# Rebuilding the head of a two-layer hybrid diffusion trunk on one core: load order, sum of squares, place of the first filter

## The chip, the core and the metric

The kernel runs on one core of one Trainium2 chip. The core has TensorE (PE in the profile; its weight loads are PEld), VectorE (DVE), ScalarE (ACT), GpSimd (POOL) and SyncE (SP), and 16 DMA engines. The metric is the device time of one launch in microseconds, the median of several runs. The whole program is one launch with fixed inputs.

## The reference, cut to what matters

Two layers work on `x` and on a context `xc`, each 256 tokens of 1024 features. The second layer leaves the context as it is.

```python
def layer_forward(x, xc, mod, mod_c, lp, update_ctx):
    sh1, sc1, g1, sh2, sc2, g2 = split(mod, 6)            # mod = silu(c) @ ada_w + ada_b
    h = modulate(rmsnorm(x, norm1_g), sh1, sc1)           # modulate: x * (1 + scale) + shift
    p = h @ w_in                                          # the context goes the same way
    attn = neighborhood_attention(q, k, v, kc, vc, rpb)   # 8 heads, softmax over 512 keys
    x = x + g1 * merge_branches(p, attn, lp)
    h = modulate(rmsnorm(x, norm2_g), sh2, sc2)
    x = x + g2 * conv_ffn(h, lp)

def merge_branches(p, attn, lp):
    a = spatial_gating_mixer(p[..., :1024])
    hy = hyena_mixer(p[..., 2560:4096])                   # two long convolutions by spectra
    g_a, g_b, g_c = split(sigmoid(p[..., 4096:]), 3)
    return (g_a * (a @ wb[0]) + g_b * (attn @ wb[1]) + g_c * (hy @ wb[2])) @ w_out

def hyena_filter_spectrum(...):
    h = sin(freq * (z @ w1 + b1)); h = sin(freq * (h @ w2 + b2))
    h = (h @ w3) * decay                                  # k: both directions
    return rfft(k / sum(abs(k)))
```

## The kernel before, in words

Activations are stored with features on the 128 partitions and tokens along the free axis: `xT` is 8 tiles of 128x512, x in columns 0 to 255 and the context in 256 to 511. Every product of layer activations and weights is done three times, with weights and activations each split in a high and a low part (`wp`, `hh`/`hl`): lines L311 to L313, or L316 to L319 where several tiles share one row of weights. The splits of weights are made some parts ahead, the high part by ScalarE (L251) and the low one by VectorE (L258). Tiles come from a pool of 77 units of 128x512, taken by `U()`; a unit taken again waits until its last reader is done.

Nothing reorders the program: each engine runs its instructions in the order in which the code issues them. Weight chunks are used one after the other in a list; after each feature tile, `pump` runs a fixed number of steps from a side queue, in which work of other parts waits as generators: the filters' spectra, spatial gating, attention, hyena. `step(g)` runs a generator to its next `yield`; `br_split` drains what a branch needs at once before its products start (spatial gating for branch 0, attention for 1, hyena for 2; their order is 0, 2, 1). Names that the text uses: `S` are attention's scores, `P` the softmax, `PT` and `PTs` its transposes and their copies, `pv` the products with the values; `Ze`/`Zo` are hyena's forward transforms, `P`, `T`, `Pp`, `Tp`, `yr`, `yi` its spectra on VectorE, `y` and `yT` its inverse transforms; `fh` are the filter's last layer, `fps` its sine layers, `nsum` its norm.

The head is `first()`. It loads x, then what the first filter needs, then the first norm's modulation weights in four groups `aw[k, c]` of 8 tiles, with weight chunks between. It squares x on ScalarE (L1241), adds the squares on POOL and VectorE (L1244), sums over partitions by four matmuls (`ssum`, L1257), takes 1/rms (L1261 and behind), spreads it over all partitions (`rb`, L1268), and forms shift and scale group by group (`gemv`, L1276 to L1286) and the normed tiles (`norm`, L1293 to L1298). Steps of the first filter are placed by hand between these. The first four feature tiles are multiplied row by row as the normed tiles come.

Of the kernel before, what the change touches and what calls it, by code (L numbers as in the profile page):

```python
# [60 lines left out]
def constants():  # L61
# [13 lines left out]
    for p in range(128):  # L75
        q = p % 64
        half, i = (q % 32) // 16, q % 16
        a = (cols if half else rows) * inv_freq[i]
        k[p, K_COS:K_COS + L] = np.cos(a)
        # rotate-half's sign comes with the sine  # L80
        k[p, K_SIN:K_SIN + L] = np.sin(a) * (-1.0 if q < 32 else 1.0)
# [12 lines left out]
def trunk_kernel(ctx: ExitStack, tc: tile.TileContext, A: dict, out: bass.AP):  # L94
# [14 lines left out]
    def fm(name, n, T, dt=F32):  # L109
        """n feature tiles of T tokens."""  # L110
# [31 lines left out]
    nc.sync.dma_start(out=prm, in_=A["prm"])  # L142
    nc.sync.dma_start(out=kst[0:33, K_POS:K_POS + 256], in_=A["kst"][0:33, K_POS:K_POS + 256])
# [31 lines left out]
    def split(src, hi, lo):  # L175
        """src = hi + lo, both with the 12 significant bits that one pass carries."""
# [12 lines left out]
    def evacuate(g):  # L189
        """an evacuation in stages: the first now, one more with each further piece of weights"""  # L190
        if g is not None and step(g):
            stages.append(g)
# [16 lines left out]
    def cuts(kind, kt, ncols):  # L209
        """a chunk's pieces in the order of their use, each cut into parts of one unit (rows k0:k1, columns c0:c1):  # L210
        a feature tile a piece (m), or all of it (t)"""
# [10 lines left out]
    def run_items():  # L222
# [39 lines left out]
        def prime(n):  # L262
            """splits n parts ahead of the next chunk"""
# [11 lines left out]
        for i, it in enumerate(items):  # L275
# [14 lines left out]
            def piece(j, more=True, i=i, qs=qs):  # L290
                """the j-th piece's rows, each in two parts; splits further parts ahead"""
# [14 lines left out]
    def mm_k(outs, W, R, k, s0, s1, n):  # L306
        """outs[i] += W[i][k]^T R[k][:, s0:s1], W and R in two parts, k of n; R's low part comes last"""
# [13 lines left out]
    def fm_run(tiles, R, s0, s1, mid=None):  # L321
        """feature tiles (W, evac, m) of one segment, side by side over the rows; mid runs ahead of their evacuation"""
# [12 lines left out]
    def fm_chunk(R, segs, evac, nm=2):  # L335
        """use() of a chunk of nm feature tiles: evac(m, ps, s0, s1) takes each."""
# [1114 lines left out]
```

## Time and profile before

| | us |
|---|---|
| three runs | 1458.31, 1463.16, 1462.58 |
| median | 1462.58 |
| span of the profiled execution | 1459.6 |
| TensorE busy | 1417.0 (97%) |
| VectorE busy | 1010.6 (69%) |
| ScalarE busy | 662.8 (45%) |
| GpSimd busy | 92.0 (6%) |

The profiled execution is known by its span alone, from its first to its last instruction. All times of rows count from the start of that span. Busy time of an engine leaves out register, branch, semaphore and DMA-issuing instructions. In rows of the timeline, a bracket such as [1.98 <-ACT hh L1295] gives the idle time of the engine ahead of the instruction and what ended it.

### The profile page before, as it was taken

What the parts mean: (1) busy time and instruction counts of PE and PEld (TensorE: products, weight loads), DVE (VectorE), ACT (ScalarE), POOL (GpSimd) and SP (SyncE); (2) the same over time, 40 slices, a digit from 0 to 9 for tenths busy, and PEclk for the clock granted to TensorE, in tenths of its full rate; (3) what the DMA queues carried; (4) which work ended last, traced back from release to release, by engine and by line L of the source; (5) the groups of instructions that cost most, each with busy time, mean ns of one, the idle gap of its engine ahead of it and who ended that gap; (6) DMA issues with size and microseconds to landing.
All of it is one profiled execution on the core that took longest, in us unless ns stands there. A gap on an engine that the chain in (4) does not pass through costs nothing.

```text
span 1459.6 us, 22459 instructions
## 1 busy us (share of the span) xinstructions
PE 1417.0 (97%) x8902; PEld 1222.7 (84%) x8902; DVE 1010.6 (69%) x1872; ACT 662.8 (45%) x1382; POOL 92.0 (6%) x96
## 2 busy tenths in 40 slices
PE   4999999999999999999999999999999999999997
PEld 3887777767878889988878787899789899999997
DVE  5736844676775566667978899587667787776574
ACT  4443332434664435533322433365436765665352
POOL 1010201010000000000011120000020000000000
PEclk9999999999999999999999999999999999999998
DMA  9934435334221523334488635535333455555642
GB/s 314 302 123 151 138 125 185 109 104 134 80 87 58 188 87 107 99 134 153 137 248 260 200 121 166 175 125 167 105 116 107 154 159 190 171 175 173 200 140 66
DMA packets 194533, 220.21 MB, mean 151 GB/s; under 512 B 5531, under 2 KB 182716, under 8 KB 189308
## 3 DMA queue, kind: packets, MB, share of 16 engines
q1 hardware_dynamic: 189420, 206.97, 43.8%
q0 software_dynamic: 2896, 9.18, 2.0%
q10 hardware_dynamic: 2112, 2.62, 0.7%
q8 instruction: 70, 1.15, 0.3%
q14 instruction: 35, 0.29, 0.1%
HBM read 215.61 MB, written 1.05 MB: 148 GB/s over the span
## 4 chain that ended last, share of the span: by engine, by line
PE 86%; DVE 7%; DMA 3%; ACT 2%; issue 1%; SPq 0%; ACTq 0%; POOL 0%; DVEq 0%; POOLq 0%
PE mm L311 23%; PE mm L313 23%; PE mm L312 23%; DVE wp L258 2%; DMA aw<-ada_w 2%; PE mt L941 2%; PE mt L943 2%; PE mt L942 2%; PE pv L815 1%; PE PT L803 1%; PE S L783 1%; PE ada L382 1%; PE Ze L643 1%; PE Zo L644 1%; PE mm L316 1%
## 5 line engine op out<-in xcount | busy, mean ns | idle before, releaser
L311 PE MATMUL mm<-hl,wp 128*128 128x256 f32 (+1 forms) x1476 | 501.1, 340 | 0.8 <-DVE hl L485 0.7
L313 PE MATMUL mm<-hh,wp 128*128 128x256 f32 (+1 forms) x1476 | 492.3, 334 | 0.0
L312 PE MATMUL mm<-hh,wp 128*128 128x256 f32 (+1 forms) x1476 | 491.9, 333 | 0.0
L258 DVE TENSOR_TENSOR wp<-w,wp 128x512 fp32r<-128x512 f32 (+1 forms) x576 | 374.6, 693 | 28.1 <-ACT wp L251 25.6
L251 ACT CAST wp<-w 128x512 fp32r<-128x512 f32 (+1 forms) x576 | 321.3, 610 | 85.8 <-DMA w<-ffn_w_down 35.5
L311 PEld LDWEIGHTS mm<-hl,wp 128*128 128x128 f32 x1476 | 281.1, 190 | 37.7 <-issue 6.6
L312 PEld LDWEIGHTS mm<-hh,wp 128*128 128x128 f32 x1476 | 281.1, 190 | 28.9 <-issue 2.9
L313 PEld LDWEIGHTS mm<-hh,wp 128*128 128x128 f32 x1476 | 280.9, 190 | 28.2 <-DVE wp L258 0.4
L311 PE MATMUL mm<-ml,wp 128*128 128x256 f32 (+1 forms) x392 | 126.1, 322 | 0.0
L313 PE MATMUL mm<-mh,wp 128*128 128x256 f32 (+1 forms) x392 | 125.4, 320 | 0.0
L312 PE MATMUL mm<-mh,wp 128*128 128x256 f32 (+1 forms) x392 | 125.4, 320 | 0.0
L311 PEld LDWEIGHTS mm<-ml,wp 128*128 128x128 f32 x392 | 74.7, 190 | 7.7 <-issue 2.4
L313 PEld LDWEIGHTS mm<-mh,wp 128*128 128x128 f32 x392 | 74.7, 190 | 5.4
L312 PEld LDWEIGHTS mm<-mh,wp 128*128 128x128 f32 x392 | 74.7, 190 | 5.2
L405 DVE SCALAR_TENSOR_TENSOR acc<-wn,scc,acc 128x512 f32<-128x512 f32 x112 | 78.3, 765 | 0.0
L1100 DVE SCALAR_TENSOR_TENSOR xT<-mm,mod,xT 128x256 f32<-128x256 f32 x72 | 33.7, 480 | 63.1 <-PE mm L313 61.5
L1134 ACT ACTIVATE a<-mm,prm 128x256 f32<-128x256 f32 (+1 forms) x48 | 30.8, 644 | 90.5 <-PE mm L313 89.5
L978 DVE SCALAR_TENSOR_TENSOR a<-mm,prm,a 128x255 f32<-128x255 f32 (+1 forms) x48 | 27.9, 581 | 57.2 <-ACT a L1134 57.2
L311 PE MATMUL mm<-bl,wp 128*128 128x512 f32 (+1 forms) x192 | 65.4, 341 | 0.0
L312 PE MATMUL mm<-bh,wp 128*128 128x512 f32 (+1 forms) x192 | 64.5, 336 | 0.0
L313 PE MATMUL mm<-bh,wp 128*128 128x512 f32 (+1 forms) x192 | 64.5, 336 | 0.0
L941 PE MATMUL mt<-wp,hh 128*128 128x256 f32 x224 | 63.8, 285 | 0.3 <-ACT va L944 0.3
(620 smaller groups left out, 2038.7 us busy)
## 6 DMA issues: line engine op xcount, KB each, us to landing
w<-w_in SPq DMA_DIRECT2D x56, 1024.0 KB, 5.1
w<-ffn_w_up SPq DMA_DIRECT2D x44, 1024.0 KB, 5.1
wn<-ada_w SPq DMA_DIRECT2D x40, 1024.0 KB, 5.0
w<-w_branch SPq DMA_DIRECT2D x24, 512.0 KB, 3.5
w<-ffn_w_down SPq DMA_DIRECT2D x16, 768.0 KB, 5.2
w<-ffn_w_down SPq DMA_DIRECT2D x16, 640.0 KB, 4.6
aw<-ada_w SPq DMA_DIRECT2D x32, 256.0 KB, 6.0
w<-w_out SPq DMA_DIRECT2D x8, 1024.0 KB, 5.3
```

Source lines behind the costliest of these rows:

```text
L251: nc.scalar.copy(h, src)
L258: vec.tensor_tensor(out=l_, in0=src, in1=spl[st["lo"]][0], op=ALU.subtract)
L311: mm(o, lhsT=wh, rhs=rl, start=(k == 0), stop=False)
L312: mm(o, lhsT=wh, rhs=rh, start=False, stop=False)
L313: mm(o, lhsT=wl, rhs=rh, start=False, stop=(k == n - 1))
L405: vec.scalar_tensor_tensor(out=o, in0=v[:, j], scalar=scc[:, k, m:m + 1], in1=o, op0=ALU.mult, op1=ALU.add)
L941: mm(o, lhsT=x, rhs=wl, start=(k == 0), stop=False)
L942: mm(o, lhsT=x, rhs=wh, start=False, stop=False)
L943: mm(o, lhsT=y, rhs=wh, start=False, stop=(k == KD - 1))
L978: vec.scalar_tensor_tensor(out=yv[:, :, 1:256], in0=pv[:, :, 0:255], scalar=w[:, 0:1], in1=yv[:, :, 1:256], op0=ALU.mult, op1=ALU.add)
L1100: vec.scalar_tensor_tensor(out=xs, in0=ps[:, s * 256 - s0:(s + 1) * 256 - s0], scalar=mod[l][:, gate_t + t, s:s + 1], in1=xs, op0=ALU.mult ...
L1134: act(out=y, in_=ps[:, 0:s1 - s0], func=AF.Identity, scale=w[:, 1:2], bias=b)
```

## The change

The parameters and the filter's positions are loaded by ScalarE's queue instead of SP's. SP's queue starts with x; then comes modulation group 0 and two chunks of weights, then the other groups, a third chunk, the constants in one piece. The modulation weights of the first norm are stored once more as `ada_0`, so that a tile is contiguous (2 KB a partition instead of two pieces of 1 KB). TensorE sums the squares: 32 matmuls, four behind each square. The first filter's sine layers stay in the head, but in smaller steps; its loads, products, norm and spectra go to the side queue behind the spatial gating, as the second filter's, and its loads go to POOL's queue. The second `gemv` stands behind the second pair of tiles' first two rows instead of ahead of it. Comments that the change drops are not shown.

```diff
-    nc.sync.dma_start(out=prm, in_=A["prm"])
-    nc.sync.dma_start(out=kst[0:33, K_POS:K_POS + 256], in_=A["kst"][0:33, K_POS:K_POS + 256])
+    nc.scalar.dma_start(out=prm, in_=A["prm"])
+    nc.scalar.dma_start(out=kst[0:33, K_POS:K_POS + 256], in_=A["kst"][0:33, K_POS:K_POS + 256])
...
             vec.tensor_scalar(out=a, in0=a, scalar1=-PI_IN, scalar2=PI_IN, op0=ALU.max, op1=ALU.min)
+            yield
             act(out=out_, in_=a, func=AF.Sin)
...
-            (vec if first else pool).tensor_tensor(out=tot, in0=tot, in1=t, op=ALU.add)
+            pool.tensor_tensor(out=tot, in0=tot, in1=t, op=ALU.add)
...
             if l == 0:
-                start(filters([spectra.pop("rest")], [(0, 1)]))
+                start(filters([spectra.pop("sin")], [(0, 0), (0, 1)]))
...
         load_x()
-        f0 = filt_load(0, 0, nc.sync, True)
-        nc.sync.dma_start(out=kst[:, 0:K_INV], in_=A["kst"][:, 0:K_INV])
...
-                nc.sync.dma_start(out=aw[k, c].rearrange("p (h c) -> p h c", h=2), in_=src[:, :, c * 256:(c + 1) * 256])
+                nc.sync.dma_start(out=aw[k, c], in_=A["ada_0"][c, k])
...
-        g, f = filt_sin(0), filt(0, 0, f0, True)
-        sq = [U("sqt") for _ in range(KD)]
...
-        for k in range(1, 5):
-            add(pool, 0, k)
-        step(g)
-        add(vec, 5, 6)
-        add(vec, 5, 7)
-        add(vec, 0, 5)
+        g = filt_sin(0)
+        step(g)
         ps = SP("ssum")
-        for i in range(4):
-            mm(ps[:, 2 * i:2 * i + 2], lhsT=sq[0][:, i * 128:(i + 1) * 128], rhs=ones[:, 0:2], start=True, stop=True)
-        step(f)
-        step(g)
+        for k in range(KD):
+            sq = U("sqt")
+            act(out=sq, in_=xT[k], func=AF.Square)
+            for i in range(4):
+                mm(ps[:, 2 * i:2 * i + 2], lhsT=sq[:, i * 128:(i + 1) * 128], rhs=ones[:, 0:2], start=(k == i == 0),
+                   stop=(k == KD - 1 and i == 3))
+        act(out=warm, in_=epsd, func=AF.Sqrt)
...
             run(W, 0, 2, 0, 2)
-            ctl["prime"](1)
-            step(f)
+            W.append(piece(0, False))
+            run(W, 2, 4, 0, 2)
             gemv(1)
             norm(2)
-            W.append(piece(0, False))
-            run(W, 2, 4, 0, 2)
             norm(3)
...
-LOADAT = (1, 2, 0, 0)                       # weight chunks loaded behind each group of layer 0's modulation
+LOADAT = (2, 0, 0, 0)
```

TensorE's program in the head, from its first matmul, before the change (`ada` are the gemv's products, `mm` the layer's):

```order
L502 MATMUL fps<-kst,prm 64x256
L502 MATMUL fps<-fs,prm 64x256
L1257 MATMUL ssum<-ones,sqt 128x2 x4
L555 MATMUL fh<-w3h,hs 128x512
L556 MATMUL fh<-w3l,hs 128x512
L555 MATMUL fh<-w3h,hs 128x512
L556 MATMUL fh<-w3l,hs 128x512
L1268 MATMUL rb<-diag,ones 128x512
L1276 MATMUL ada<-aw,scc 32x128 x32
L555 MATMUL fh<-w3h,hs 128x512
L556 MATMUL fh<-w3l,hs 128x512
```

And in the changed kernel, from the same place:

```order
L502 MATMUL fps<-kst,prm 64x256
L1231 MATMUL ssum<-ones,sqt 128x2 x32
L1241 MATMUL rb<-diag,ones 128x512
L1250 MATMUL ada<-aw,scc 32x128 x32
L316 MATMUL mm<-hh,wp 128x512
```

The eight `fh` and the second `fps` left this place, and `ssum` has eight times as many matmuls.

TensorE's program where layer 0's attention ends, ahead of the gate chunk (`mm` with `bl`, `bh` are a branch's products, with `hl`, `hh` the gate's), before the change:

```order
L311 MATMUL mm<-bl,wp 128x512
L312 MATMUL mm<-bh,wp 128x512
L313 MATMUL mm<-bh,wp 128x512
L815 MATMUL pv<-PTs,va 64x128 x4
L311 MATMUL mm<-hl,wp 128x512
```

And in the changed kernel, at the same branch product:

```order
L313 MATMUL mm<-bh,wp 128x512
L807 MATMUL pv<-PTs,va 64x128 x8
L795 MATMUL PT<-ident,P__4321 128x128 x4
L795 MATMUL PT<-ident,P__4330 128x128 x4
L807 MATMUL pv<-PTs,va 64x128 x8
L775 MATMUL S<-K__4033,Q__4131 128x256 x2
L775 MATMUL S<-K__4041,Q__4138 128x256 x2
L795 MATMUL PT<-ident,P__4395 128x128 x2
L795 MATMUL PT<-ident,P__4403 128x128 x2
L807 MATMUL pv<-PTs,va 64x128 x4
```

Behind these rows stand, once more, two scores, two transposes and `pv`, and then the gate's first product. Before, the last scores, transposes and values of the attention stood between the branch's products.

VectorE's program in hyena's first order, from a spectrum's middle to the inverse transform's operands (L1054 before, L1046 now, is the evacuation of a branch tile), before the change:

```order
L657 TENSOR_TENSOR yr<-Pp,K 128x512
L658 TENSOR_TENSOR yi<-Pp,K 128x512
...
L666 TENSOR_TENSOR P<-yr 128x512
L667 TENSOR_TENSOR T<-yi 128x512
L668 TENSOR_TENSOR Pp<-yr 128x512
L669 TENSOR_TENSOR Tp<-yi 128x512
L178 TENSOR_TENSOR bl<-u,bh 128x512 x4
```

And in the changed kernel:

```order
L258 TENSOR_TENSOR wp<-w,wp 128x512
L1046 SCALAR_TENSOR_TENSOR m<-gt,mm 128x512
L649 TENSOR_TENSOR yr<-Pp,K 128x512
L650 TENSOR_TENSOR yi<-Pp,K 128x512
...
L258 TENSOR_TENSOR wp<-w,wp 128x512
L1046 SCALAR_TENSOR_TENSOR m<-gt,mm 128x512
L658 TENSOR_TENSOR P<-yr 128x512
L659 TENSOR_TENSOR T<-yi 128x512
L660 TENSOR_TENSOR Pp<-yr 128x512
L661 TENSOR_TENSOR Tp<-yi 128x512
```

The spectra of the first order now stand among the evacuations of branch tiles, behind the split of the branch's operand (`bl`) instead of ahead of it.

## Rows read from the trace of the kernel before

**Rows 1.** The page: busy time of the engines, and TensorE's in 40 slices.

```profile
PE 1417.0 (97%) x8902; PEld 1222.7 (84%) x8902; DVE 1010.6 (69%) x1872; ACT 662.8 (45%) x1382; POOL 92.0 (6%) x96
...
PE   4999999999999999999999999999999999999997
```

**Rows 2.** Windows: from:to, length, busy time by engine, granted clock, DMA share, GB/s.

```profile
0.00:17.30 17.30, 2.19 (x4) 0.57 (x4) 9.40 (x24) 8.73 (x16) 5.78 (x10) 1.00 0.91 276
17.30:41.07 23.77, 18.12 (x170) 12.52 (x171) 16.25 (x38) 8.76 (x18) 0.52 (x1) 1.00 1.10 348
7.00:10.00 3.00, 0.44 (x1) 0.29 (x2) 1.03 (x3) 2.69 (x6) 1.98 (x2) 1.00 1.03 386
14.00:22.00 8.00, 4.67 (x14) 3.41 (x14) 6.90 (x16) 3.30 (x6) 0.00 (x0) 1.00 1.10 352
```

**Rows 3.** Timeline of TensorE in the head: start, busy us, instruction, idle before.

```profile
17.34 1.87 PE L1257 MATMUL ssum<-ones,sqt 128*128 128x2 f32 x8 [6.66 <-DVE sqt L1244]
...
20.49 0.63 PE L556 MATMUL fh<-w3l,hs 128*128 128x512 f32 x1
20.91 1.91 PE L1268 MATMUL rb<-diag,ones 128*128 128x512 f32 x2
22.75 2.90 PE L1276 MATMUL ada<-aw,scc 128*32 128x128 f32 x64
...
26.15 0.39 PE L555 MATMUL fh<-w3h,hs 128*128 128x512 f32 x1
26.38 0.39 PE L556 MATMUL fh<-w3l,hs 128*128 128x512 f32 x1
28.46 0.50 PE L316 MATMUL mm<-hh,wp 128*128 128x512 f32 x1 [1.69 <-ACT wp L251]
...
32.10 1.95 PE L1276 MATMUL ada<-aw,scc 128*32 128x128 f32 x64
```

**Rows 4.** Tile ssum in the head: duration min/median/max in ns, first and last start.

```profile
L1257 PE MATMUL ssum<-ones,sqt x8: 352/352/373, 17.3 to 18.8; 128*128 128x2 f32 x8
```

**Rows 5.** Timeline of ScalarE in the head.

```profile
3.88 1.28 ACT L371 ACT_TABLE_LOAD   x1 [3.88 <-DMA prm<-prm]
...
5.93 0.63 ACT L1241 ACTIVATE sqt<-xT 128x512 f32<-128x512 f32 x1 [0.54 <-DMA xT<-xT]
...
11.93 0.63 ACT L1241 ACTIVATE sqt<-xT 128x512 f32<-128x512 f32 x1 [0.40 <-DMA xT<-xT]
```

**Rows 6.** Two windows around a fall of the granted clock, and TensorE between.

```profile
570.00:577.70 7.70, 6.93 (x54) 6.32 (x53) 6.41 (x17) 4.70 (x11) 0.00 (x0) 1.00 0.01 2
577.70:581.10 3.40, 3.40 (x19) 3.40 (x18) 2.54 (x6) 2.92 (x5) 0.00 (x0) 0.50 0.00 0
...
576.18 0.95 PE L458 MATMUL ssum<-ones,sqt 128*128 128x2 f32 x8
```

**Rows 7.** Timeline of VectorE and TensorE where the head's last hole ends.

```profile
36.58 2.29 DVE L568 TENSOR_TENSOR tot<-tot,abs 128x512 f32<-128x512 f32 x3 [0.36 <-ACT abs L567]
...
41.07 0.50 PE L316 MATMUL mm<-hh,wp 128*128 128x512 f32 x1 [1.98 <-ACT hh L1295]
```

**Rows 8.** Hyena's last spectrum and inverse on TensorE; a wait from 312 to 330.

```profile
311.06 1.02 PE L643 MATMUL Ze<-tm,kst 128*128 128x512 f32 x2
...
328.44 0.46 PE L690 MATMUL yT<-kst,P 128*128 128x128 f32 x2 [1.68 <-DVE P L666]
...
ACT wp L251 <- DVE yr L661: 5.8, 1, 5.8
```

**Rows 9.** Timeline of the attention's last group: scores, softmax, copies, values.

```profile
474.74 0.51 PE L783 MATMUL S<-K__3866,Q__3979 128*128 128x256 f32 x2
...
476.54 0.36 DVE L796 TENSOR_SCALAR P__4370<-P__4370,sm 128x256 f32<-128x256 f32 x1
...
478.54 0.65 ACT L805 COPY PTs<-PT 128x256 f32<-128x256 f32 x2 [1.27 <-PE PT L803]
...
481.34 0.66 PE L815 MATMUL pv<-PTs,va 128*64 128x128 f32 x8
```

More of the change, by code (lines that the diff above doesn't have):

```diff
@@ L510, in layer @@
             vec.tensor_scalar(out=a, in0=a, scalar1=-PI_IN, scalar2=PI_IN, op0=ALU.max, op1=ALU.min)
+            yield
             act(out=out_, in_=a, func=AF.Sin)
-        layer(w1, kst[0:33, K_POS:K_POS + 256], b1, h)
+        yield from layer(w1, kst[0:33, K_POS:K_POS + 256], b1, h)
         yield
-        layer(w2, h, b2, h)
-        yield
+        yield from layer(w2, h, b2, h)
         split(h, hs[0:64, :], hs[64:128, :])
@@ L524, in inv, with filt_load @@
         return kst[:, K_INV + 128 * i:K_INV + 128 * (i + 1)]
-    def filt_load(l, n, q, later=False):
+    def filt_load(l, n, q):
         dec = [U("dec") for _ in range(2)]
@@ L536, in filt_load, with filt @@
             q.dma_start(out=dec[i], in_=A["dec"][:, i, :])
-        def load_skip():
-            q.dma_start(out=skip, in_=A["hy_skip"][l, n:n + 1, :].to_broadcast([128, 512]))
-        if not later:
-            load_skip()
-        return dec, w3, skip, load_skip
-    def filt(l, n, loaded, first=False):
+        q.dma_start(out=skip, in_=A["hy_skip"][l, n:n + 1, :].to_broadcast([128, 512]))
+        return dec, w3, skip
+    def filt(l, n, loaded):
         K = spectra.setdefault(l, [])
-        dec, w3, skip, _ = loaded
+        dec, w3, skip = loaded
         hd, w3s = {}, []
@@ L560, in filt @@
         pool.memset(hd[1, 0][0:1, :], 0.0)
-        if first:
-            yield
         tot = U("tot")
@@ L567, in filt @@
             act(out=t, in_=hd[de], func=AF.Abs)
-            (vec if first else pool).tensor_tensor(out=tot, in0=tot, in1=t, op=ALU.add)
-        if first:
-            yield
+            pool.tensor_tensor(out=tot, in0=tot, in1=t, op=ALU.add)
         sd = {}
@@ L1228, in first @@
                 aw[k, c] = U("aw")
-                src = A["ada_w"][0, k * 128:(k + 1) * 128, 0:2048].rearrange("p (h c) -> p h c", h=2)
-                nc.sync.dma_start(out=aw[k, c].rearrange("p (h c) -> p h c", h=2), in_=src[:, :, c * 256:(c + 1) * 256])
+                nc.sync.dma_start(out=aw[k, c], in_=A["ada_0"][c, k])
             if LOADAT[c]:
                 ctl["load"](LOADAT[c])
-        f0[3]()
         ctl["load"](RAWB)
         silu_c()
-        g, f = filt_sin(0), filt(0, 0, f0, True)
-        sq = [U("sqt") for _ in range(KD)]
-        def square(k0, k1):
-            for k in range(k0, k1):
-                act(out=sq[k], in_=xT[k], func=AF.Square)
-        def add(eng, a, b):
-            eng.tensor_tensor(out=sq[a], in0=sq[a], in1=sq[b], op=ALU.add)
-        square(0, 4)
-        step(g)
-        square(4, KD)
-        for k in range(1, 5):
-            add(pool, 0, k)
-        step(g)
-        add(vec, 5, 6)
-        add(vec, 5, 7)
-        add(vec, 0, 5)
-        ps = SP("ssum")
-        for i in range(4):
-            mm(ps[:, 2 * i:2 * i + 2], lhsT=sq[0][:, i * 128:(i + 1) * 128], rhs=ones[:, 0:2], start=True, stop=True)
-        step(f)
-        step(g)
+        g = filt_sin(0)
+        step(g)
+        ps = SP("ssum")
+        for k in range(KD):
[5 more added lines that the diff above has]
+        act(out=warm, in_=epsd, func=AF.Sqrt)
         r = small.tile([128, 8], F32, tag="rn", name="r")
@@ L1305, in first @@
         norm(1)
-        step(f)
         ctl["prime"](2)
-        spectra["rest"] = f
-        nc.sync.dma_start(out=kst[:, K_INV:K_POS], in_=A["kst"][:, K_INV:K_POS])
+        spectra["sin"] = g
+        nc.sync.dma_start(out=kst[:, 0:K_POS], in_=A["kst"][:, 0:K_POS])
         for l in range(DEPTH):
@@ L1326, in use_b @@
             run(W, 0, 2, 0, 2)
-            ctl["prime"](1)
-            step(f)
+            W.append(piece(0, False))
+            run(W, 2, 4, 0, 2)
             gemv(1)
             norm(2)
-            W.append(piece(0, False))
-            run(W, 2, 4, 0, 2)
             norm(3)
@@ L1338, in use_b @@
             norm(5)
-            step(f)
+            step(spectra["sin"])
             run(W, 0, 4, 4, 5)
@@ L1342, in use_b @@
             norm(6)
-            step(f)
             run(W, 0, 4, 5, 6)
@@ L1346, in use_b @@
             run(W, 0, 4, 6, 7)
-            step(f)
             ctl["prime"](4)
@@ L1378 @@
 HYY = (1, 1)
-LOADAT = (1, 2, 0, 0)
-_NAMES = ["xT", "prm", "kst", "dec", "ada_w", "w_in", "sgu_w", "sgu_norm_g", "sgu_b", "rpb", "hy_filt_w3", "hy_skip",
+LOADAT = (2, 0, 0, 0)
+_NAMES = ["xT", "prm", "kst", "dec", "ada_w", "ada_0", "w_in", "sgu_w", "sgu_norm_g", "sgu_b", "rpb", "hy_filt_w3", "hy_skip",
           "w_branch", "w_out", "ffn_w_up", "ffn_w_down"]
@@ L1414, in layout @@
     r["ada_w"] = i["ada_w"]
+    r["ada_0"] = i["ada_w"][0, :, 0:2048].reshape(8, 128, 2, 4, 256).transpose(3, 0, 1, 2, 4).reshape(4, 8, 128, 512)
     idx = np.arange(IN_COLS)
```

## The prediction

> **What bounds the kernel now.** I read the page first: TensorE is busy 97% of the span, VectorE 69%, and only the first and the last of the 40 slices show TensorE below nine tenths [rows 1]. So there are two places where a change of order can pay or cost: the head, where TensorE idles, and the stretches in which another engine is nearly late. The table of windows over the head comes next: TensorE works 2.19 us of the first 17.3 and 18.12 of the 23.77 behind them, up to 41.07 [rows 2]: 20.8 us idle there, of 42.6 in the whole span (1459.6 less 1417.0). The head is what the change rewrites, and it can give back at most a part of that.
>
> Why is TensorE idle there? The timeline shows that the sums of squares (ssum) start at 17.34, waiting for VectorE's additions; then come rb, the first gemv (ada) at 22.75, and the first product of the layer at 28.46 [rows 3]. The last square on ScalarE ran at 11.93 [rows 5], so 5 us of that lie in POOL's and VectorE's additions, beside VectorE's own filter work. DMA is full: 386 GB/s while x comes in rows of 2 KB, 352 while the modulation weights come in rows of 1 KB [rows 2].
>
> **The head, step by step.** Parameters on ScalarE's queue let x start at once. A tile of 256 KB takes 0.68 us at 386 GB/s, and the first was there at 5.93 [rows 2, 5]; the changed modulation group (contiguous rows of 2 KB, as x) comes at x's pace, so 8 x tiles end near 10.7, group 0 near 16, the two weight chunks (8 x 256 KB) near 21.5. Before, filter loads of 1.3 MB and 0.5 MB of constants stood between, and group 0 landed near 22.5. That is 6 us earlier, and DMA no longer ends last.
>
> What ends last instead is TensorE's own sum. Eight passes took 1.87 us, with starts from 17.3 to 18.8, so 0.2145 us a pass [rows 3, 4]. The change has 32 matmuls where there were 4, so 64 passes: 64 x 0.2145 = 13.7 us. They begin when the first square is done: parameters near 4.4 (x now shares the transfers; 3.88 before), table load 1.28, square 0.63 [rows 5], and a Silu of 16 columns that I put at 0.3: near 6.6. The end is 20.3, against 19.2 before: 1.1 us later. This rests on the clock. These passes run at the low one of its two levels: behind them an fh pass of 512 columns still takes 0.42 us to the next start (20.49 to 20.91), while at 26.15 it takes 0.23 [rows 3]. That is 1.2 and 2.4 GHz (the granted clock reads full in both, so I go by the pitch). gemv 0 takes 2.90 where gemv 1 takes 1.95, so it began at the low clock and ended at the high one: with 3.9 all low, c + (3.9 - c) / 2 = 2.9 gives c = 1.9, a rise near 24.65. Would 13.7 us of ssum raise it sooner? The one instance that I can read speaks against it: near 577.7 the granted clock fell to half directly behind a stretch in which TensorE was 6.93 of 7.70 us busy and whose last work was short products, holes and eight ssum passes [rows 6]. I take no rise until gemv.
>
> The Trainium skill (TensorE: Matmul & The Clock Gate, Part 1: What's actually happening) says that the clock follows how busy TensorE has recently been. By the letter of it, gap-free ssum passes would raise the clock; the fall at 577.7 speaks against it here, and the case is a rival below.
>
> From ssum's end the chain is as before: r, reciprocal, four diagonals 1.7 us (19.2 to rb's 20.91), rb 1.84, gemv 2.9 [rows 3]: gemv ends near 26.8. From gemv's end (25.6) to the first product it was 2.8: near 29.7, against 28.46. After it, the order is kinder: twelve products, then twelve of the second pair, then gemv 1, whose weights are long there, and VectorE's three additions to tot (2.29 us up to 38.87, straight ahead of the norm for which TensorE waits until 41.07 [rows 7]) are gone from it. That norm still needs 2.2 us (38.87 to 41.07) behind gemv 1, on whose end TensorE has nothing else to do. Before, the twelve, gemv 1 and the twelve took 9.0 us with 1.7 of waits for weights (28.46 to 32.10, 1.95, 3.3); now 29.7 + 3.6 + 3.4 + 1.95 + 2.2, and a wait for the second pair's splits of about 1, is near 41.9. Head: **+1**, range -9 (DMA the bound and the clock high from the start: that row near 32) to +3 (weight splits late by 2 more).
>
> **What leaves the head lands on a busy engine.** The eight fh products cost nothing before, since they ran while rb and the first norm waited [rows 3]. Behind the spatial gating TensorE is full: 8 x 0.23 = 1.84, and two passes of 256 columns for the sine's second layer, 0.4 by the same pitch and their start: **+2.3**, with no cover. If that stretch had idle time I don't see, it is 0. The first norm sum has 52 products (12 us) between it and fh, which covers its additions on POOL. ScalarE's two more table loads (1.28 each) fall where it is 45% busy [rows 1]: nothing. POOL's queue takes six more loads behind the gating: if late, they cost up to 1; I take 0.
>
> **Everything behind the filter comes five feature tiles later.** The side queue runs one step a tile. Filter (0,0) takes seven steps where the remainder took two, so the second filter, the hyena and the attention of layer 0 slide by five. That costs at two places.
>
> *Hyena.* The unit pool is nearly empty in this stretch: one weight cast already waits 5.8 us for VectorE's yr to free a unit [rows 8]. Before, the last spectrum started at 311.06, TensorE did 52 products, and the inverse yT still waited 1.68 for VectorE up to 328.44 [rows 8]: 17.4 us are needed from spectrum to yT, 15.7 were there. In the new order two pairs have 52 products between, one of them with VectorE's y work split around the gate tiles, whose evacuations wait for TensorE. By 17.4 against 15 the waits are 2.4 each; the casts and products there that wait for a unit released 16 to 44 products before use (51 was the least before) add up to 2 on the first. So 4.3 and 2.4 and a small 0.5, less the old 1.68: **+5.5**, range 2 (two bare waits) to 8.
>
> *Attention.* The branch split drains it. Before, one group of four pv stood there, at 481.34, with no idle time around [rows 9]. Now the tail is: pv, two PT, pv, then twice (scores, transposes, pv) with no product of the layer between. In normal flow this latency is covered: scores at 474.74, P ready at 476.90, copies PTs at 478.54, pv at 481.34, all beside products [rows 9]. Back to back it is bare. For each of the two last groups: scores to P 2.16, TensorE busy 0.46 of it, so 1.7; then transpose to copy about 0.5, two copies 0.65 together, less some 0.45 busy, so 0.7: 2.4 each. For the first, with 512 keys, the copies are twice as wide, 0.65 each by that row: 0.8 bare. Sum **+5.6**, range 4 (some softmax under way) to 9 (VectorE and ScalarE late with gate evacuations). With these holes TensorE idles about as much as before the fall at 577.7 [rows 6], where 3.4 us ran at half clock and lost 1.7; I give that two chances in three: 1.7 x 0.65 = **+1**.
>
> **Sum.** 1 + 2.3 + 5.5 + 5.6 + 1 = +15.4. The profiled execution's span is 1459.6; the page gives no further time for it, and its runs took 1458.31 to 1463.16 with a median of 1462.58. So 1475 by the span and 1478 by the median: I take **1477**.
>
> **Rivals.** A time within 0.3% (4.4 us) cannot be told from no change.
>
> *1. The head really gives time.* If ssum counts as work, the clock rises as in the old head 7.3 us after it starts (17.34 to 24.65 then, 6.6 to 13.9 now); 34 passes are done, the rest cost 0.107 each, ssum ends at 17.1 and rb and gemv run at the high clock. First product at 24.8, head -4: 1472, still slower. With squares faster still and DMA the bound the head gives -9. Then with hyena and attention at their low ends (+2, +4) and 2.3 moved, -0.7: 1462, same. Chance of the same band 0.14.
>
> *2. Faster.* It needs head -9 and the drained attention hidden: if softmaxes of the tail run ahead of TensorE so that burst and hyena cost below 2.3 together, the sum falls under -4.4: 1457. Against it stands that the scores themselves are in the burst, and that TensorE executes in order; it decides at side costs under 4.6 in all. Chance 0.10.
>
> *3. Worse.* Half-clock stretches follow both hyena waits and the burst, and the units run out so that weights come late: head +3, hyena 8, attention 9, three stretches of 1.7, and 2.3: +27, 1489. Chance 0.12.
>
> My case has the rest, 0.64: 1467 to 1484 by itself. The range reaches over the same case and most of the worse one: **1460 to 1489**. Slower 0.76, same 0.14, faster 0.10.
>
> **What would show it.** Right: ssum passes at 0.21 to 0.23 us to about 20; the first product near 30; a row of idle holes on TensorE before the gate chunk near 485, waiting for P and PTs; yT and y waiting for VectorE's P for 2 to 4 us. Wrong: ssum at half that pitch or ended by 13; the first product before 25; the attention tail without holes. If the whole loss sits in the head, my side shift is wrong; if the head is 5 us or more shorter, my clock is.

## The result, and the profile after

The changed kernel takes 1486.07 us (median of four runs, 1483.61 to 1489.0) where the kernel before takes 1461.44 (four runs, 1458.31 to 1463.16): 24.6 us more, a ratio of 1.0177 with a 95% interval of 1.0163 to 1.0191. It is slower, as forecast, and inside the range; the sum said +15.4, so its size was too small by 9.

The page of the changed kernel first, in the lines that answer to [rows 1]: the span, busy time by engine, TensorE's busy tenths in 40 slices.

```profile
span 1487.2 us, 22585 instructions
PE 1441.4 (97%) x8958; PEld 1241.5 (83%) x8958; DVE 1007.7 (68%) x1866; ACT 666.9 (45%) x1385; POOL 96.3 (6%) x102
PE   7999999989999999999999999999999999999997
```

The shares are nearly those of before; the first slice went from 4 up to 7, and the ninth, in hyena, fell to 8. TensorE is busy 24.4 us longer (1441.4 against 1417.0), and its idle time, span less busy, grew by only 3.2 (45.8 against 42.6). So most of the loss is hidden in "busy". To find it I cut both executions at the same products of the layer (the 48th, 456th, 1008th, 1176th and 1640th): head, first tiles, filters, hyena, attention, rest. These are the windows of the changed kernel (bounds, length, busy us and count by engine, granted clock, DMA share, GB/s):

```profile
0.00:52.70 52.70, 40.48 (x310) 32.44 (x310) 20.46 (x57) 18.15 (x34) 0.69 (x6) 0.90 1.01 351
52.70:134.35 81.65, 81.65 (x529) 69.33 (x529) 40.55 (x72) 31.95 (x63) 8.61 (x16) 1.00 0.48 156
134.35:286.11 151.76, 147.46 (x742) 109.53 (x740) 89.55 (x135) 59.11 (x119) 25.93 (x20) 0.99 0.39 136
286.11:350.26 64.15, 59.77 (x253) 41.13 (x249) 41.24 (x63) 15.85 (x27) 5.92 (x5) 0.95 0.30 99
350.26:511.57 161.31, 154.23 (x853) 123.07 (x849) 110.02 (x231) 87.32 (x219) 10.69 (x11) 0.97 0.30 95
511.57:1487.20 975.63, 957.86 (x6285) 866.01 (x6283) 705.87 (x1312) 454.48 (x925) 44.50 (x46) 0.99 0.47 150
```

And the same stretches of the kernel before, which no row above shows:

```profile
0.00:50.36 50.36, 29.60 (x263) 20.46 (x263) 32.12 (x76) 20.80 (x39) 7.79 (x12) 0.97 1.03 326
50.36:134.92 84.56, 84.56 (x544) 71.18 (x542) 43.27 (x78) 33.46 (x65) 5.01 (x9) 1.00 0.51 175
134.92:284.16 149.24, 147.93 (x760) 110.82 (x759) 89.34 (x137) 52.67 (x110) 20.98 (x16) 1.00 0.43 142
284.16:339.73 55.57, 53.61 (x242) 38.73 (x241) 41.11 (x61) 15.31 (x28) 8.50 (x7) 1.00 0.33 107
339.73:483.90 144.17, 143.79 (x820) 115.57 (x817) 96.98 (x211) 85.33 (x217) 4.81 (x6) 1.00 0.31 98
483.90:1459.60 975.70, 957.54 (x6285) 865.94 (x6283) 707.77 (x1313) 455.24 (x926) 44.94 (x46) 0.99 0.47 151
```

Subtract the lengths: head +2.3, first tiles -2.9 (pieces of the first filter that stood there are gone), filters +2.5, hyena +8.6, attention +17.1, rest -0.1. The head is not shorter, and everything else is lost in layer 0 behind it. Where a row of before has a granted clock of 1.00, hyena and attention now have 0.95 and 0.97.

The head's timeline on TensorE answers to [rows 3, 7] (start, us, instruction, in brackets the idle time ahead and what ended it):

```profile
6.57 13.81 PE L1231 MATMUL ssum<-ones,sqt 128*128 128x2 f32 x64 [0.72 <-ACT sqt L1229]
21.96 2.07 PE L1241 MATMUL rb<-diag,ones 128*128 128x512 f32 x2 [1.58 <-DVE diag L1239]
23.96 2.83 PE L1250 MATMUL ada<-aw,scc 128*32 128x128 f32 x64
29.60 0.79 PE L316 MATMUL mm<-hh,wp 128*128 128x512 f32 x1 [2.81 <-ACT wp L251]
...
38.45 1.96 PE L1250 MATMUL ada<-aw,scc 128*32 128x128 f32 x64
42.75 0.70 PE L316 MATMUL mm<-hh,wp 128*128 128x512 f32 x1 [2.35 <-ACT hh L1269]
```

The sum starts at 6.57 instead of 17.34, and the first product of the layer comes at 29.60 instead of 28.46: the 64 passes of the sum fill what was idle and end at 20.38. TensorE's idle time in the head fell from 20.8 to 12.2 us, and its own work took the place.

Behind the head the list of TensorE's waits (who waited for whom, us in total, times, longest), from 134.35 to 511.57, shows what the shift of the side queue did:

```profile
PE y L668 <- DVE P L658: 4.3, 2, 3.8
PE PT L795 <- DVE sm L787: 3.8, 4, 1.6
PE nrm L583 <- DVE tot L578: 2.0, 1, 2.0
PE yT L682 <- ACT wp L251: 2.0, 1, 2.0
PE fh L552 <- DVE w3l L178: 1.2, 1, 1.2
...
PE fh L551 <- ACT w3h L177: 0.4, 1, 0.4
```

In the kernel before, the same list between the same products has a single wait over 1 us, the yT of [rows 8]. The list names a weight cast on ScalarE as what ended yT's wait; yT reads P, which VectorE formed up to the same moment (yT starts at 363.40):

```profile
362.57 0.69 DVE L658 TENSOR_TENSOR P<-yr 128x512 f32<-128x512 f32 x1
```

The tail of attention, the drained burst that answers to [rows 9]:

```profile
499.45 0.50 PE L775 MATMUL S<-K__4033,Q__4131 128*128 128x256 f32 x2
...
501.75 0.41 PE L795 MATMUL PT<-ident,P__4395 128*128 128x128 f32 x2 [1.56 <-DVE sm L787]
...
502.68 1.05 PE L807 MATMUL pv<-PTs,va 128*64 128x128 f32 x8
...
506.25 0.66 PE L795 MATMUL PT<-ident,P__4431 128*128 128x128 f32 x2 [1.36 <-DVE sm L787]
...
507.37 1.57 PE L807 MATMUL pv<-PTs,va 128*64 128x128 f32 x8
508.87 0.80 PE L311 MATMUL mm<-hl,wp 128*128 128x512 f32 x1
```

The last two groups of scores have no product of the layer beside them, and TensorE waits for the softmax as forecast. Two rows alike show one more thing: the same pv takes 1.05 at 502.68 and 1.57 at 507.37. The granted clock fell in between, to its low level (0.50 in the rows, 1.2 GHz; 1.00 is 2.4). These are the stretches at that level up to the end of attention, by windows:

```profile
29.22:36.05 6.83, 6.45 (x15) 4.75 (x16) 6.59 (x13) 4.87 (x10) 0.00 (x0) 0.50 1.06 388
42.88:46.29 3.41, 3.41 (x9) 2.64 (x10) 2.00 (x5) 0.91 (x2) 0.00 (x0) 0.50 1.09 355
158.93:162.34 3.41, 3.41 (x6) 1.59 (x5) 0.36 (x1) 1.62 (x3) 0.00 (x0) 0.50 0.84 335
333.01:339.84 6.83, 6.11 (x8) 2.52 (x9) 4.28 (x7) 1.62 (x3) 0.00 (x0) 0.50 0.72 230
363.73:367.14 3.41, 3.36 (x15) 3.03 (x14) 2.53 (x5) 0.09 (x1) 0.00 (x0) 0.50 0.40 137
503.68:510.51 6.83, 5.47 (x21) 3.83 (x21) 2.51 (x8) 3.56 (x11) 0.00 (x0) 0.50 0.59 192
```

Each lies behind or around a hole in TensorE's work: the wait ahead of the first product up to 29.60, that for hh up to 42.75, nrm's at 157.6, y's at 333.7, yT's at 363.4, the burst. The kernel before had one such stretch up to there, of 3.4 us at 41.8. I price a stretch at half of TensorE's busy time in it, an estimate: a product of 512 columns follows the one before after 0.43 us in the stretch at 29.22 and after 0.23 outside. That gives 9.2 us for the four behind the head, and 4.9 in the head against 1.7 before. The clock's share depends on the execution: the four of this kernel had spans of 1481.8 to 1487.2 at granted clocks of 0.991 to 0.984, and the profiled one is the longest.

### The profile page after: what moved, and what is told of

Its sections match the earlier page's. It is cut to its first block, busy times and chain, and to the rows that moved or that the text cites. A ratio compares the mean times of both kernels' runs of the same rounds, so it can differ in the third digit from the quotient of the medians.

```text
span 1487.2 us, 22585 instructions
## 1 busy us (share of the span) xinstructions
PE 1441.4 (97%) x8958; PEld 1241.5 (83%) x8958; DVE 1007.7 (68%) x1866; ACT 666.9 (45%) x1385; POOL 96.3 (6%) x102
## 3 DMA queue, kind: packets, MB, share of 16 engines
HBM read 215.61 MB, written 1.05 MB: 146 GB/s over the span
## 4 chain that ended last, share of the span: by engine, by line
PE 68%; DVE 10%; ACT 3%; issue 1%; ACTq 0%; DVEq 0%
PE mm L311 19%; PE mm L312 19%; PE mm L313 19%; DVE wp L258 2%; PE pv L807 1%; PE PT L795 1%; PE mt L933 1%; PE mt L935 1%; PE mt L934 1%; PE S L775 1%; DVE mx L782 1%; PE Zo L636 1%; PE Ze L635 1%; ACT wp L251 1%; PE yT L683 1%
```

## The experiments

Two theories. **Side queue:** the loss comes from the first filter's seven steps going into an in-order side queue, which makes everything behind them five feature tiles late, so that waits lose their cover, and the clock falls in them. **Head:** the sums on TensorE are what costs, and the side queue does little. Each ratio is to runs of the kernel before that were taken beside it (medians of 1459.89 to 1461.19).

**The side queue put back in step.** Five feature tiles of layer 0 run one more side step, before hyena begins:

```diff
-            pump(int(ctl["due"]))
+            ctl["tile"] = ctl.get("tile", -99) + 1
+            pump(int(ctl["due"]) + (ctl["tile"] in EXTRA))
...
+EXTRA = (8, 11, 15, 16, 17)
```

> The changed kernel, with one more step of the side queue behind five of the feature tiles in which the two filters run, so that hyena and attention of layer 0 stand again where they stood before the change; the filter's work stays behind the gating. My theory (the loss is the five tiles by which hyena and attention are late): the holes before the gate chunk and at y go, with the half-clock stretches behind them, and of 24.6 us some 20 come back: 1466, 1463 to 1470. Rival 1 (the filter's work itself on a full TensorE, and its own waits, is the loss): at least 1478. Rival 2 (the head is the loss): 1484 to 1487.

1471.64 us, ratio 1.0072 (1.0057 to 1.0087). Nothing else of the change was touched, and 14.4 of the 24.6 us are back, less than the 20 expected. Its windows from filters to attention:

```profile
132.58:292.40 159.82, 155.18 (x781) 114.95 (x780) 100.75 (x155) 59.33 (x120) 27.50 (x21) 0.99 0.40 132
292.40:349.55 57.15, 55.19 (x242) 40.12 (x240) 41.12 (x61) 15.31 (x28) 8.54 (x7) 0.97 0.32 106
349.55:493.70 144.15, 143.78 (x820) 115.57 (x817) 96.94 (x211) 85.47 (x217) 4.79 (x6) 1.00 0.30 98
```

Attention takes what it took before (144.15 against 144.17), and hyena all but 1.6. The filters take 10.6 more than before, of which 2.9 had left the first tiles: there the filter's own products and waits stay (fh 1.38 and 1.16, two nsum 1.01 and 0.69). From the head's end to attention's end it is 442.8 us against 433.5 before: even in step, the filter, with its waits and two low stretches, costs 9.2 us on a busy TensorE.

**The move alone.** In the kernel before, only the first filter is moved behind the spatial gating; sums, queues and load order stay:

```diff
-        f0 = filt_load(0, 0, nc.sync, True)
...
-        g, f = filt_sin(0), filt(0, 0, f0, True)
+        g = filt_sin(0)
...
-                start(filters([spectra.pop("rest")], [(0, 1)]))
+                start(filters([iter(())], [(0, 0), (0, 1)]))
```

> The kernel before, with the first filter's loads, products, norm and spectra moved behind the gating and nothing else changed: old load order of x and modulation, old sums of squares. My theory: nearly the whole loss is there, 1461 + 24 = 1485, less up to 3 for the 1.3 MB that leave the head's full DMA queue: 1481 to 1486. Rival 2 (64 ssum passes and the new head are the loss): 1460 to 1465.

1482.41, ratio 1.0149 (1.0131 to 1.0167). The head got shorter, 45.64 against 50.36, but its first product comes no earlier (28.58 against 28.46): what is gone is work behind it, 3.2 of it TensorE's own (26.41 busy against 29.60). From there to attention's end it is 458.0 against 433.5, +24.4. So this one part is worth the loss behind the head. Its head is also 5 to 7 us shorter than the changed kernel's (50.8 to 52.7 in its profiles), and its median 3.7 us, with intervals that overlap at their ends: the new sums and load order do not pay here, and may cost.

**Adding on VectorE.** Squares are added by seven VectorE instructions, four matmuls instead of 32; the rest as changed:

```diff
+        sq = [U("sqt") for _ in range(KD)]
         for k in range(KD):
...
+            act(out=sq[k], in_=xT[k], func=AF.Square)
+            if k:
+                vec.tensor_tensor(out=sq[0], in0=sq[0], in1=sq[k], op=ALU.add)
```

> The changed kernel, with the squares added by seven operations of VectorE and four ssum matmuls instead of 32. My theory (TensorE's 64 passes at 0.2145 us set the head's end): ssum ends near 14 instead of 20.4, the first layer product starts 5 to 7 us earlier, and the time falls by as much: 1479, 1477 to 1482. Rival (what is gained in the head is lost again at the next wait, for the weights' splits or the second modulation group): 1484 to 1487.

1483.4, ratio 1.0151 (1.0132 to 1.017), which overlaps the changed kernel's interval: missed. The sum now starts at 14.13 and the first product at 26.02, 3.6 earlier than changed. The profiled execution was the shortest of its four (1479.95, the others up to 1484.96), so its span of 1478.2 says little about the median. By the medians the narrow sums on TensorE cost some 3 us against these additions, which isn't clear of the noise; they aren't the bulk.

**The filter kept in the head.** The changed kernel's queues, load order and sums on the kernel before, whose filter keeps its place in the head; of the change only the lines on the filter are left out. Its core, against the kernel before:

```diff
-    nc.sync.dma_start(out=prm, in_=A["prm"])
+    nc.scalar.dma_start(out=prm, in_=A["prm"])
...
+                nc.sync.dma_start(out=aw[k, c], in_=A["ada_0"][c, k])
...
+            if c == 0:
+                f0 = filt_load(0, 0, nc.sync, True)
...
+            square(k, k + 1)
+            for i in range(4):
+                mm(ps[:, 2 * i:2 * i + 2], lhsT=sq[k][:, i * 128:(i + 1) * 128], rhs=ones[:, 0:2], start=(k == i == 0),
+                   stop=(k == KD - 1 and i == 3))
```

> The changed kernel's head (queues, packed group first, sums by TensorE, gemv order), but with the first filter kept in the head as before, its loads behind the first two weight chunks. My theory: only the head's own +1.7 us is left, 1463, 1460 to 1467, with fh and the sine layer hidden again in TensorE's waits. Rival (the head's order also costs later on, through the clock or the units): 1475 or more.

1475.25, ratio 1.0097 (1.008 to 1.0114): missed by 12 us. The head went wrong and the rest right. The windows of filters, hyena and attention:

```profile
144.98:294.35 149.37, 147.94 (x760) 110.83 (x759) 89.34 (x137) 52.64 (x110) 20.95 (x16) 1.00 0.43 142
294.35:350.27 55.92, 53.61 (x242) 38.74 (x241) 41.46 (x61) 15.30 (x28) 8.50 (x7) 1.00 0.32 107
350.27:494.45 144.18, 143.80 (x821) 115.57 (x818) 96.99 (x211) 85.40 (x217) 4.80 (x6) 1.00 0.31 97
```

The squares stand behind the first sine on ScalarE, so the sum starts at 9.77; fh then waits for hs until 30.38, rb behind it on the same engine, and the first product comes at 39.12. From the first tiles to attention each stretch is that of before within 0.4 us. Together with the three runs above this settles the first theory: filter in the head, no loss behind; filter moved, 23 to 25 us behind in the profiles with three different heads, 9 when the queue is in step.

**Filter in the head, additions on VectorE.** Meant to take the best of both:

```diff
-                start(filters([spectra.pop("sin")], [(0, 0), (0, 1)]))
+                start(filters([spectra.pop("rest")], [(0, 1)]))
...
+            step(f)
+            step(f)
             run(W, 0, 4, 2, 3)
```

> The changed kernel with the squares added by VectorE and with the first filter back in the head, behind the first products: fps behind the sums, fh in the hole ahead of the third row of products, nsum behind the seventh, two steps left for the side queue, so that everything behind stands as before the change. The fourth experiment started its sums late and lost 10 us in the head, and lost nothing behind it. My theory (the side queue's delay is the loss, and the new load order by itself is a gain): the head ends 4 us or more earlier than before, and the time is under the kernel before: 1456, 1453 to 1460. Rival (the filter's loads and splits hold up the head again): 1462 to 1470.

1472.17, ratio 1.0081 (1.0064 to 1.0097): missed. The head has new holes, 4.0 us from 32.78, where weight splits stand behind the second sine on ScalarE, and 3.7 from 45.94, where fh waits for VectorE; the head is 10.2 us longer than before (60.51).

**Sums by wide products.** Eight matmuls of ones with whole squares, 512 columns each, put the sum on all partitions at once; rb and the diagonals fall away, and 1/rms is taken on 128x512:

```diff
-            for i in range(4):
-                mm(ps[:, 2 * i:2 * i + 2], lhsT=sq[:, i * 128:(i + 1) * 128], rhs=ones[:, 0:2], start=(k == i == 0),
-                   stop=(k == KD - 1 and i == 3))
+            mm(ps, lhsT=ones, rhs=sq, start=(k == 0), stop=(k == KD - 1))
...
-        mm(rb, lhsT=ones, rhs=dg, start=True, stop=True)
+        rb = U("rb")
+        act(out=rb, in_=ps, func=AF.Sqrt, scale=1.0 / D, bias=epsd)
+        vec.reciprocal(out=rb, in_=rb)
```

> The changed kernel, with eight matmuls of 512 columns against a square of ones in place of 32 of two columns, which gives the sum on all partitions at once; root and reciprocal are taken on 128x512, and rb's matmul and the diagonals go. Theory (passes of two columns leave the clock low, wide ones raise it): the passes start at about 0.85 to 0.95 us and end at half of that, the sums end near 16 instead of 20.4, gemv runs in 1.95, the first product starts near 23 to 24, and the time falls by 4 to 7: 1480 to 1483. Rival (the clock stays low until gemv whatever the passes are): sums end at 21, first product at 27 to 30, 1484 to 1488.

1479.26, ratio 1.0126 (1.0109 to 1.0144), about 7 us less than changed. The head's timeline, with VectorE's reciprocal:

```profile
6.62 9.32 PE L1230 MATMUL ssum<-sqt,ones 128*128 128x512 f32 x16 [0.70 <-ACT sqt L1229]
15.87 1.95 PE L1243 MATMUL ada<-aw,scc 128*32 128x128 f32 x64
...
16.70 3.35 DVE L1234 RECIPROCAL rb<-rb 128x512 f32<-128x512 f32 x1 [7.89 <-ACT rb L1233]
...
22.64 0.80 PE L316 MATMUL mm<-hh,wp 128*128 128x512 f32 x1 [4.82 <-ACT wp L251]
```

Sixteen passes of 512 columns take 9.32 us where 64 of 2 columns took 13.81, and the gemv behind them takes 1.95, not 2.83: the clock is at its high level when it starts. The first product comes 7 us earlier than changed, though the wait ahead of it is longer (4.82 against 2.81): the gemv is done at 17.82, but VectorE takes up its result at 19.97, behind the reciprocal, and the norm and the weight cast that is named stand behind that. The loss behind the head stays.

**Holes of attention filled.** Six products of 512 columns, whose results nobody reads, behind each of the last two groups of scores:

```diff
+            if r and ctl.get("fill"):
+                ps = SP("fill")
+                for i in range(6):
+                    mm(ps, lhsT=K[pr, 0][:, 0:128], rhs=K[pr, 0], start=(i == 0), stop=(i == 5))
```

> The changed kernel, with six additional products of 512 columns (their result is not used) behind each of the last two groups of scores, in the holes in which TensorE waits for the softmax; nothing else moves. Theory (the 6.8 us at half clock that begin at 503.7 come from these holes): the holes of 1.56 and 1.36 us are filled at no cost, no half-clock stretch follows, and 2 to 3.4 us come back: 1483, 1481 to 1485. Rival (the clock falls for the short transposes and values, not for the holes): the stretch stays, 1486 to 1489.

1485.96, ratio 1.0167 (1.015 to 1.0184): not told from the changed kernel, and between the two expectations. In its profile the two holes shrank:

```profile
499.80 0.41 PE L799 MATMUL PT<-ident,P__4395 128*128 128x128 f32 x2 [0.17 <-DVE sm L791]
...
504.02 0.41 PE L799 MATMUL PT<-ident,P__4438 128*128 128x128 f32 x2 [0.19 <-DVE sm L791]
```

The transposes run at 0.41, so the clock is high here and the stretch at 503.7 is gone; another of 3.4 us stands at 600.75, which the changed kernel doesn't have. As executions of one kernel differ in their stretches, this single profile can't say that the filling did it.

**Steps of attention joined.** Five pairs of attention's steps are run as one, so that the tail drains as before, and only the tail is in step again:

```diff
-            yield
+            if l or i not in (8, 10, 14, 16, 20):
+                yield
```

> The changed kernel; only five of layer 0's attention steps, those without scores, are joined with the step that follows, so that attention catches up five tiles by its end and the branch split drains four pv again and no scores. Hyena stays as late as in the changed kernel. Theory (the drained tail costs its holes of 3.2 us, the 6.8 us at half clock and the bare latencies): 6 to 9 us come back: 1478, 1476 to 1481. Rival (the waits only move into the joined steps): 1484 to 1488.

1487.52, ratio 1.0179 (1.0162 to 1.0196): no gain. From the 1176th to the 1640th product TensorE now idles 6.8 us, against 7.1 changed:

```profile
350.09:508.59 158.50, 151.68 (x852) 122.18 (x849) 109.02 (x230) 85.56 (x218) 10.65 (x11) 0.99 0.28 90
```

The holes of the tail are gone and stand inside the joined steps instead (1.55 before a pv at 429.41, three pairs of about 0.5 and 0.3 before transposes). The reading that the tail itself is what costs fell. What fits is that with five tiles less of products the same waits have less cover wherever they stand; no run varies that cover by itself.

**Wide sums with the filter in the head.** First the edits of the fifth and sixth experiments together (filter in the head, wide sums instead of the additions):

> The fifth experiment with the sixth's wide sums in place of VectorE's additions. Theory: if wide passes raise the clock, the head ends some 1 to 4 us earlier than the fifth's: 1453, 1449 to 1458. Rival (clock stays low through the sums): 2 to 5 us later than the fifth.

1474.01, ratio 1.0089 (1.0074 to 1.0104): missed too: the head is 57.11 long, and by its profile the holes behind the first products decide, not the sum. Then the changed kernel with wide sums and the filter's steps put, one by one, where the profile of the sixth kernel has idle time (sine steps in and behind the first products, fh behind gemv 1, its norm between the next tiles):

```diff
+            step(g)
             run(W, 2, 4, 0, 2)
+            step(g)
+            step(f)
             gemv(1)
             norm(2)
+            step(f)
             norm(3)
+            step(f)
```

> The changed kernel's load order with the wide sums of the sixth experiment, and the first filter back in the head with its pieces where the engines have room by that profile: its loads behind modulation group 1, its second sine layer behind the weights' splits, fh in the hole ahead of the third row of products with its evacuations between the two norms, additions, differences and norm as in the kernel before. Two steps are left for the side queue, so everything behind stands as before the change. Theory (the side queue's delay and the narrow sums are the whole loss): the head ends 5 to 8 us earlier than before, nothing is lost behind it: 1455, 1452 to 1458. Rival (the filter holds up the head wherever it stands, as in the fourth and fifth): 1462 to 1472.

1463.3, ratio 1.0018 (1.0009 to 1.0026): 8 us over what was expected, in the rival's range. The head is 45.84 long, 4.5 less than before, filters, hyena and attention 149.31, 56.68 and 144.16; but the first tiles take 87.44, 2.9 more (1.73 of it holes at 53.55 and 58.07), and later stretches at low clock, at 1071.65 and 1143.33, may take some of the rest: the kernel before has none there.

**The same, additions on VectorE behind a warm-up.** Twelve passes of x with ones that nobody reads (six products of 512 columns), then squares added on VectorE and eight narrow passes:

```diff
+        ps = SP("wide")
+        for i in range(6):
+            mm(ps, lhsT=ones, rhs=xT[0], start=(i == 0), stop=(i == 5))
```

> The ninth experiment with three edits to its head. Its profile shows a reciprocal of 128x512 of 3.35 us behind the wide sums, so the squares are added by VectorE and summed by eight narrow passes, as in the third; six wide products of x with ones, whose result is not used, stand ahead of them on TensorE; and the first filter's split of its weights and its differences move to where VectorE has room. Theory (wide work on TensorE raises the clock whatever it is for): ssum runs at 0.11 us a pass, rb and gemv at the high clock, the first layer product starts near 21 against 22.3 in the ninth, and holes of 2 to 3 us at 33 and 53 to 59 go: 1459, 1456 to 1461. Rival (weights or modulation groups bound the head at that point): 1462 to 1464, as the ninth.

1460.64 against 1460.78, ratio 1.0001 (0.9992 to 1.0009): the same as before. So the 24.6 us are got back in full, but no version beat the kernel before. It also splits the filter's weights ahead of the second sine. Its sum in the timeline:

```profile
4.49 7.37 PE L1234 MATMUL wide<-xT,ones 128*128 128x512 f32 x12 [4.49 <-DMA xT<-xT]
12.83 1.05 PE L1242 MATMUL ssum<-ones,sqt 128*128 128x2 f32 x8 [0.97 <-DVE sqt L1240]
```

The eight narrow passes take 1.05 us here, where they took 1.87 [rows 3].

**Both repairs on the changed kernel.** Side queue in step and wide sums, the edits of the first and sixth experiments together:

> The first and the sixth experiment together: the changed kernel with five joined side steps and wide sums; the filter stays behind the gating. If the side queue's delay and the narrow sums are separate losses, their gains add: 1471.6 less 6.8 is 1465, 1462 to 1468, and what is left over the kernel before is the filter's own work and waits on a full TensorE. If not (the head's gain is lost at the filter's waits): 1469 to 1473.

1467.28, ratio 1.0034 (1.0021 to 1.0048). The gains nearly add: 1.05 and 0.51 points off 1.77 would leave 0.21, and 0.34 are left. So the two causes are mostly separate.

## Why the prediction was right, and where its size was off

The time lies in the stated range, but near its upper end and above the 1467 to 1484 that the prediction gave its own case by itself: the mechanism held, and one term above all, the clock, was far too small. Its terms, with what the two profiled executions give between the same products (span +27.6):

| term | forecast | measured |
|---|---|---|
| head | +1 | +2.3 |
| moved work, no cover | +2.3 | +4.1 |
| waits in the filters | 0 | +2.8 |
| waits of hyena | +5.5 | +4.7 |
| waits of attention | +5.6 | +4.6 |
| clock behind the head | +1 | +9.2 |
| sum | +15.4 | +27.7 |

Moved work is busy time less half the low-clock time, from the first tiles to attention: 433.9 against 429.9. Not all of it is moved products: by the same count the first experiment, with the same products, gives +2.6, near the forecast, and the sine's second layer still ran in the head, at 52.13. The rest of the 4.1 is not accounted for. Each row of waits is the idle time on TensorE in its own instructions, less that of before: hyena's yT and y, attention's PT and pv, the filter's nrm, fh and nsum.

**The head: right.** The sum was to end at 20.3, gemv at 26.8, the first product to come at 29.7, the third row at 41.9; they stand at 20.38, 26.79, 29.60 and 42.75. That the 64 passes would not raise the clock, the step on which the first rival hung, was right: they took 13.81 us without a hole, 0.216 a pass, at the low level to the end. The trace has its first entry on the clock, at the high level, at 25.81, in the gemv, and the kernel before at 24.74, where the prediction had worked out 24.65. The Trainium skill (TensorE: Matmul & The Clock Gate, Part 1: What's actually happening) says that the clock follows how busy TensorE has recently been; by the busy time of the rows this trace doesn't agree, since 13.81 us of narrow passes left it low, and the run with wide ones does, its first entry at the high level standing at 11.05, in the sum. Not foreseen was the low stretch at 29.22, behind the 2.81 us wait ahead of the first product, half of whose 6.45 busy us is lost. Three experiments have the same head: with a shorter stretch there it is 50.93 and 50.81 long (side queue in step, holes filled), with the same one 52.60 (steps joined). So the term is +0.5 to +2.3 by execution.

**The side queue: right, shown by four runs.** Put in step, the tail and most of hyena's loss are gone; moved alone, the whole of it is there; with the filter in the head (two runs), none. Waits of hyena and attention came within 1 us of their terms each. In hyena, y's wait of 3.77 and yT's of 1.96 stand where 4.3 and 2.4 were forecast, and small ones besides. Attention's sum is in part luck: the tail waited 3.2 us in all, not 5.6 (1.56 and 1.36 for the softmax instead of 2.4 each, 0.24 instead of 0.8), and 1.3 us more than before, which the prediction did not have, fell ahead of it. And the drained tail is not needed for the loss: with attention's steps joined its holes went and the time stayed.

**What failed.** The step "I give that two chances in three: ... +1" for the clock. It saw one place, the drained tail, and one stretch of 3.4 us; the trace has a stretch behind four of the holes, two of them 6.8 us long. The rival that counted three such stretches came nearest in the whole (1489), but with waits of 8 and 9 us that were not there and 5.1 for the clock, which was more. Then the waits in the filters were put at nothing: "POOL's queue ... I take 0" looked for a delay in the loads, and the first norm's sum was taken to be covered by 52 products. Both were so: the loads of w3 were issued by 102.1 and landed within 8 us, long before the split at 137, and nsum did not wait. What was left out is what stands behind the evacuations and weight splits of the feature tile in progress: nrm waited 1.98 us for its diagonals (tot) on VectorE, and the second filter's first fh waited 0.44 for ScalarE's cast of w3 and 1.16 for VectorE's low part of it. VectorE in those microseconds:

```profile
153.56 1.28 DVE L258 TENSOR_TENSOR wp<-w,wp 128x512 fp32r<-128x512 f32 x2
...
155.54 0.75 DVE L972 SCALAR_TENSOR_TENSOR pc<-mm,prm,pc 128x510 f32<-128x510 f32 x1
156.20 0.16 DVE L575 TENSOR_SCALAR rn<-nsum 128x8 f32<-128x8 f32 x1
...
156.70 0.87 DVE L578 TENSOR_SCALAR tot<-ident,rn 128x128 f32<-128x128 f32 x4
...
177.18 1.28 DVE L178 TENSOR_TENSOR w3l<-w,w3h 128x512 fp32r<-128x512 f32 x2
```

TensorE's nsum was done at 154.66; rn stands behind a weight split and two evacuations until 156.20. The split of w3 stands behind two evacuations until 177.18; the fh that needs it starts at 177.92. With 2.8 and 8.2 these two steps make up 11 of the 12.3 us by which the terms fell short. The first experiment divides the loss by cause instead: the five tiles' delay is worth 14.4 us by the medians, where hyena, attention and the clock were forecast at 12.1, and the filter in step 9.2 in the profile, where 2.3 were. The profiled execution has the clock's share at its largest: the shortest of the four is 5.4 us shorter at 0.991.

**What stays open** is why a hole is followed by a low stretch in one execution and not in another; the traces show only where.

## What to carry to other kernels

Work deferred into an in-order side queue cost much more here than its own time: list each wait behind it with the cover it has, and look for what now drains with no cover, before counting what the head gains; here putting the queue back in step afterwards got 14.4 of 24.6 us back with a few lines of code. Waits on a busy TensorE should be priced with the low-clock time behind them, here 9.2 us on 12.1 us of waits. Idle time filled with narrow passes is no gain if these passes sit on the path; wide ones did the same sum in two thirds of the time and left the clock high.

## What was not expected of the hardware

64 passes of two columns without a hole left TensorE at the low level of its clock for all of their 13.81 us. Eight of them took 1.87 [rows 3] and, behind twelve wide ones at the high level, 1.05, while the granted clock reads 1.00 in either stretch. The traces have no entry on the clock ahead of its first rise (24.74 in the kernel before, 25.81 in the changed one, 8.48 with the warm-up), and a row counts time without an entry as 1.00; up to there the pitch of passes tells the level. A reciprocal of 128x512 on VectorE took 3.35 us, where the one of 128x8 takes 0.20; with it the first norm, and so the wide sum's first product, comes some 2 us later.
